# Out-projection operands on another queue, a first block without marks, and a reordered end in a hybrid encoder layer

## The chip, the cores and the metric

The kernel runs on one core of a Trainium2 chip. The metric is the device time of one execution in microseconds (us). Three runs of the kernel before took 2081.64, 2083.21 and 2086.21 us; the median is 2083.21. A profile was taken of a further execution, which took 2080.18 us, with 2078.4 us from its first to its last instruction (the span). All rows of the trace come from that execution.

Engines have short names in the profile: PE is TensorE, PEld its weight loads, DVE VectorE, ACT ScalarE, POOL GpSimd, SP SyncE, which here only issues DMAs. A name with q (SPq, ACTq, POOLq) is the instruction queue of an engine. L207 is line 207 of the kernel.

## What is computed

One layer of an encoder, on two sequences with the same weights: the prompt (512 tokens) and the sample (1024 tokens). The width is 2048, everything is float32.

```
def mixer_layer(x, ...):
    h = rms_norm(x, norm_g)
    c_val, c_glu, c_gate, q, k, v, a_gate = split(h @ w_in)
    q, k = rope(q), rope(k)
    conv_out = conformer_conv(c_val, c_glu, ...) * silu(c_gate)    # 31 taps, layer norm, silu, @ w_pw
    attn_out = banded_sink_attention(q, k, v, sink) * silu(a_gate) # 8 heads, 2 kv heads, window 128
    return x + concat([conv_out, attn_out]) @ w_out

y = rms_norm(mixer_layer(x, ...), final_norm_g)     # for both sequences
```

The final norm divides each row by the root of its mean square and multiplies it by a gain. For the sum `x + ... @ w_out` the kernel must add products to rows that lie in memory; much of the change is about how those rows are fetched.

## The kernel before

**Products.** Each float32 operand is split into a high part and a low part (`parts`, L506: ACT copies the high part, L510, or L514 with a factor; DVE subtracts to get the low part, L511 or L515). A product is then three TensorE passes: high by high, high by low, low by high. For most of the work the blocks are also combined as in Strassen's scheme: seven products P1 to P7 (a `Unit`) in place of eight, on sums of weight blocks and sums of token blocks. One product of a unit is twelve TensorE instructions of 128x512 (L207). The order within a unit is P1, P2, P6, P5, P7, P3, P4 (`ALONE`). P1, P6, P7 and P4 share one bank of the accumulator, so P6 goes on in the bank of P1 after P1's value was taken out (`tap`). The remaining products, those of the prompt's in-projection, are plain (`Job`, L669): 48 instructions each for one block of 128 columns, from two prepared weight blocks.

**Stages.** In order of time: the sample's in-projection as units in four passes (the first by `Plain`, L349); the prompt's in-projection as jobs, with the sample's attention slipped between them (L1167 scores, L1201 transposes, L1196 values); the point-wise product of the convolution for the sample; the sample's out-projection in units of the class `Onto`; then the prompt's point-wise product and its out-projection with the final norm (`LastPost`), written out by hand in `last_run`.

**Onto.** A unit of the out-projection takes a tile from memory for each of its four output quarters (`begin`, L282 to L285, from `x` in the first half of the contraction, from the stored partial sum, `part_out`, in the second), adds the accumulator to it (`tap`, L304) and stores it. A load is asked for `ahead` products before the product that needs it; `ahead` is 2, and 0 for the first two units of the second half, `over[1][:2]`, which run side by side (each product of one, then the same product of the other, on the banks a, b, c and s, s, pt). The unit before asks for the first tile of the next one if `next` is set. The tiles alternate between two rings of four buffers, G and U (`E`, L477). There are 8 pairs of columns, hence 16 units and 64 such loads. They are issued by SP, on whose queue stand nearly all other DMAs as well: weights (L123, L127, L404), token blocks (L878), stores (L504), the attention's queries (L1148).

**Order of the queues.** Each engine works through a list of instructions that is fixed when the kernel is built. The builder goes through the program and takes, for each engine, the ready instruction of highest priority; `urgently` and `high_priority(URGENT)` lift instructions, and `issue_after(i)` keeps an instruction behind `i` on the same engine. `mark` (L523) notes the last DVE and ACT instructions so far, and whatever is built inside `behind()` stays behind these. Lanes (attention, convolution, preparation) are generators that are advanced a little after each group of products (`tick`). An instruction that waits holds up all that stands behind it on its engine.

**Weights.** `w_prep` and `w_prep_now` (L625, L631) prepare the next block: load (`raw`), high and low part (`hl`, three buffers). A `Prep` may be marked `behind`. For the prompt's first job, `pj[0]`, `behind` and `early` are set (L2020), so both its blocks (`k` = 0 and `k` = 8) are made behind the marks. The unit ahead of it, `end = stages[3][-1]` (L2013), looks `NHL - 1` = 2 blocks ahead.

**Landing.** In the last pass of the sample's in-projection a finished quarter is completed by an adding DMA on POOL from the stored part (`add_into`, L501); what follows on it (`done`; for the gates a DVE multiplication, L974, an ACT silu, L982, and a store from ACT's queue, L983) is put in `later` with a count, `landing` = 4. `turn_over` (L542), called once a product, lowers the counts and builds the next step of an entry that has come to zero. Before each job, entries that are left are built at once (L656).

**Start.** `constants` (L561) loads `norm_g` through SP ahead of everything; `first` (L1886) loads the first weights and tokens in small pieces, and 20 spin products (`warm`, L1904, L559) run meanwhile.

**End.** In `last_run`, four row blocks of the prompt (128 rows of 2048) lie in SBUF in two halves (`rows[b][0]`, `rows[b][1]`), each half in interleaved column blocks, even and odd. The last product, P4, adds to the row blocks 2 and 3, one after the other (`finished`, `tap`, `add`, L1726). `complete` (L1728) takes the sum of squares (L1735); on the fourth and last part of a row block it works out the inverse root (L1745 to L1750, a root and one step of correction), scales both halves, each by one ACT and one DVE instruction (L1754, L1756, L1758), and stores each half as it is done (L1759, 512 KB).

Of the kernel before, what the change touches and what calls it, by code (L numbers as in the profile page):

```python
# [7 lines left out]
F32 = mybir.dt.float32  # L8
F32R = mybir.dt.float32r
AF = mybir.ActivationFunctionType  # L10
# [260 lines left out]
class Onto(Unit):  # L271
# [10 lines left out]
    def begin(self, n):  # L282
        if n not in self.d:
            self.d[n] = self.e.E()
            self.e.nc.sync.dma_start(self.d[n], self.source(*n))  # L285

# [99 lines left out]
class Job:  # L386
# [10 lines left out]
    def preps(self, e):  # L397
        def one(k):
# [26 lines left out]

            return Prep(load, make, behind=self.behind)

# [3 lines left out]
class Encoder:  # L431
# [129 lines left out]
    def constants(self):  # L561
# [6 lines left out]

        self.norm_g = load("norm_g", [ND])
        self.ones = self.const.tile([P, P], F32, name="ones")  # L570
# [986 lines left out]
class LastPost(Post):  # L1557
# [136 lines left out]
    def load_rows(self):  # L1694
        e = self.e
        half = D // 2
        self.half = half
        self.rows = [[None, None] for _ in range(NB)]
        self.gain = {}
        self.sq = [e.small(4) for _ in range(NB)]  # L1700
        self.rest = [e.small(1) for _ in range(NB)]
        self.load_columns(0, e.A)

# [24 lines left out]
    def complete(self, b, c, odd):  # L1728
# [5 lines left out]
        junk = e.G().rearrange("p (i x) -> p i x", x=P)  # L1734
        nc.scalar.activation(junk, y, AF.Square, accum_out=self.sq[b][:, n : n + 1])  # L1735
        if n < 3:
            nc.vector.tensor_tensor(y, y, self.gain[c, odd], ALU.mult)
        sq, rest = self.sq[b], self.rest[b]
        if n == 2:
            nc.vector.tensor_tensor(rest, sq[:, 0:1], sq[:, 1:2], ALU.add)  # L1740
            nc.vector.tensor_tensor(rest, rest, sq[:, 2:3], ALU.add)
            nc.vector.tensor_scalar(rest, rest, 1.0 / D, RMS_EPS, ALU.mult, ALU.add)
        if n == 3:
            s, v, t = e.small(1), e.small(1), e.small(1)
            nc.scalar.activation(s, sq[:, n : n + 1], AF.Sqrt, scale=1.0 / D, bias=rest)  # L1745
            nc.vector.tensor_scalar(v, sq[:, n : n + 1], 1.0 / D, rest, ALU.mult, ALU.add)
            nc.vector.reciprocal(s, s)
            nc.vector.scalar_tensor_tensor(t, s, s, v, ALU.mult, ALU.mult)
            nc.vector.tensor_scalar(t, t, -0.5, 1.5, ALU.mult, ALU.add)
            nc.vector.tensor_tensor(s, s, t, ALU.mult)  # L1750
            half = self.half
            for h in range(2):
                other, last = (self.blocks(self.rows[b], h, o) for o in (1 - odd, odd))
                nc.scalar.activation(other, other, AF.Identity, scale=s)  # L1754
                if h == c:
                    nc.vector.scalar_tensor_tensor(last, last, s, self.gain[c, odd], ALU.mult, ALU.mult)  # L1756
                else:
                    nc.vector.tensor_scalar(last, last, s, None, ALU.mult)  # L1758
                nc.sync.dma_start(self.out[b * P : (b + 1) * P, h * half : (h + 1) * half], self.rows[b][h])  # L1759

# [14 lines left out]
    def last_run(self, at):  # L1775
# [5 lines left out]
        for c in range(2):  # L1781
            bank = [None] * 3
            for name in ENDS[c]:
# [25 lines left out]
                if end:  # L1809
# [3 lines left out]
                    parts = {m: e.hl.pop(at + self.place[c, name, m]) for m in self.PAIRS}  # L1813
                    for args in pending:
                        e.urgently(self.complete, *args)
                    pending.clear()
                    for t in range(2):
                        for m in self.PAIRS:
                            for i in range(2):
                                products(t, m, i, parts[m][i])  # L1820
                        finished(t)
                        e.urgently(self.complete, *pending.pop())
                    continue
# [34 lines left out]
def encoder(ctx, tc, a):  # L1858
# [27 lines left out]
    def first():  # L1886
# [16 lines left out]
        e.w_load(3)  # L1903
        e.warm(20, True)  # L1904
        sums = sample.first_sums(x)
# [107 lines left out]
    end = stages[3][-1]  # L2013
    end.look = NHL - 1
    end.before.append(last_before)
# [72 lines left out]
    for u in over[1][:2]:  # L2088
        u.ahead = 0
    over[1][0].next = None  # L2090
# [69 lines left out]
```

## Time and profile before

| what | value |
|---|---|
| timed runs, us | 2081.64, 2083.21, 2086.21 |
| the profiled execution, us | 2080.18 |
| its span, us | 2078.4 |
| mean granted TensorE clock | 0.997 |
| TensorE busy, us | 2060.7 |
| VectorE busy, us | 1754.4 |
| ScalarE busy, us | 1043.6 |
| GpSimd busy, us | 122.6 |
| mean DMA rate, GB/s | 238 |

In the rows of a timeline the first number is the start in us from the beginning of the span, the second the time in us; then engine, line, operation, result <- operands, shape and count of what was merged into the row. In brackets stands the idle time of the engine just ahead of it, and what ended it. A row of waits gives: engine, tile and line that waited, after the arrow what it waited for, then us in total, number of times, and the longest. A row of a stretch gives the busy time of each engine in it, the granted share of TensorE's clock, the share of the DMA engines that was busy, and GB/s. In a list of a line's instructions, three numbers with slashes are minimum, median and maximum, in ns; "DMA to landing" has them in us.

### The profile page before, as it was taken

The page shows a single profiled execution, that of the slowest core. Times are in us where ns is not written, and L with a number is a line of the kernel's source. Part 1 is how long each engine was busy: PE and PEld are TensorE (multiplying, and loading weights), DVE is VectorE, ACT ScalarE, POOL GpSimd, SP SyncE. Part 2 cuts the span into 40 slices and gives each one's busy share as a digit, 9 for nine tenths or more (in the row PEclk, how much of TensorE's full clock was granted, in tenths as well). Part 3 has the DMA queues.
Part 4 walks back from the last instruction along what each step waited for, and adds up shares of the span by engine and source line. Part 5 has one row for each costly group of instructions (what it writes and reads, how often), then busy time and mean ns, then how long its engine had stood idle before and what let it go on. Part 6 is the DMA issues. An engine that isn't in the chain of part 4 may idle for free.

```text
span 2078.4 us, 27092 instructions
## 1 busy us (share of the span) xinstructions
PE 2060.7 (99%) x9259; PEld 1699.2 (82%) x9259; DVE 1754.4 (84%) x2873; ACT 1043.6 (50%) x1711; POOL 122.6 (6%) x176
## 2 busy tenths in 40 slices
PE   9999999999999999999999999999999999999998
PEld 8888888888888888788888888888888887888886
DVE  8767899998899999999666877767799977998887
ACT  7485445333464434554455777336454343454454
POOL 0111111111111111100000000000000000000000
PEclk9999999999999999999999999999999999999999
DMA  8888886864577767954455555996789899678897
GB/s 288 312 298 256 199 223 221 285 220 160 188 242 192 175 169 183 280 166 156 153 172 187 177 182 183 315 330 234 247 289 300 278 299 293 220 247 298 289 333 277
DMA packets 245819, 494.55 MB, mean 238 GB/s; under 512 B 23600, under 2 KB 84400, under 8 KB 245680
## 3 DMA queue, kind: packets, MB, share of 16 engines
q1 hardware_dynamic: 225136, 445.62, 63.9%
q0 software_dynamic: 19392, 45.10, 9.4%
q10 hardware_dynamic: 1152, 2.10, 0.3%
q8 instruction: 72, 1.18, 0.2%
q14 instruction: 67, 0.55, 0.1%
HBM read 331.77 MB, written 160.96 MB: 237 GB/s over the span
## 4 chain that ended last, share of the span: by engine, by line
PE 48%; DVE 7%; issue 6%; DMA 4%; ACT 2%; POOL 1%; SPq 0%; ACTq 0%; POOLq 0%; DVEq 0%
PE a L669 13%; PE a L207 7%; PE c L669 6%; PE b L669 6%; PE c L207 3%; PE pv L1196 2%; PE a L1835 2%; PE s L1167 2%; PE s L1835 2%; PE b L207 1%; PE pt L1201 1%; DVE hl L511 1%; DVE f L1003 1%; DVE t L511 1%; DVE f L1040 1%
## 5 line engine op out<-in xcount | busy, mean ns | idle before, releaser
L207 PE MATMUL a<-t,hl 128*128 128x512 f32 x2640 | 633.6, 391 | 4.7 <-DVE u L304 3.2
L207 PEld LDWEIGHTS a<-t,hl 128*128 128x128 f32 x2640 | 494.7, 188 | 110.6 <-DVE u L304 3.6
L510 ACT ACTIVATE hl<-raw 128x1024 fp32r<-128x1024 f32 (+3 forms) x334 | 296.1, 890 | 384.5 <-PE c L207 81.6
L511 DVE TENSOR_TENSOR hl<-raw,hl 128x1024 fp32r<-128x1024 f32 (+3 forms) x334 | 338.8, 1015 | 145.8 <-ACT hl L510 144.4
L669 PE MATMUL a<-t,hl 128*128 128x512 f32 x1344 | 328.0, 394 | 0.0
L207 PE MATMUL c<-t,hl 128*128 128x512 f32 x1320 | 319.2, 389 | 0.0
L207 PEld LDWEIGHTS c<-t,hl 128*128 128x128 f32 x1320 | 247.3, 188 | 51.6 <-DVE u L304 0.4
L669 PEld LDWEIGHTS a<-t,hl 128*128 128x128 f32 x1344 | 248.6, 188 | 49.8
L1040 DVE SCALAR_TENSOR_TENSOR f<-f,c_w_dw,f 128x512 f32<-128x512 f32 x248 | 173.9, 750 | 0.3
L669 PE MATMUL b<-t,hl 128*128 128x512 f32 x672 | 164.6, 395 | 2.2 <-DVE hl L511 2.2
L1003 DVE SCALAR_TENSOR_TENSOR f<-f,c_w_dw,f 128x512 f32<-128x512 f32 x232 | 163.7, 748 | 1.2 <-ACT f L998 1.2
L669 PE MATMUL c<-t,hl 128*128 128x512 f32 x672 | 164.2, 393 | 0.3 <-DVE hl L511 0.3
L207 PE MATMUL b<-t,hl 128*128 128x512 f32 x660 | 160.0, 389 | 0.0
L669 PEld LDWEIGHTS b<-t,hl 128*128 128x128 f32 x672 | 126.1, 190 | 28.0 <-DVE hl L511 2.6
L669 PEld LDWEIGHTS c<-t,hl 128*128 128x128 f32 x672 | 124.7, 188 | 25.5 <-DVE hl L511 0.7
L207 PEld LDWEIGHTS b<-t,hl 128*128 128x128 f32 x660 | 123.7, 188 | 25.6
L1032 DVE SCALAR_TENSOR_TENSOR f<-f,w_both,f 128x512 f32<-128x512 f32 x120 | 90.0, 750 | 2.1
L236 ACT ACTIVATE u<-a 128x512 f32<-128x512 f32 x82 | 48.7, 594 | 66.8 <-PE a L207 64.2
L236 ACT ACTIVATE g<-a 128x512 f32<-128x512 f32 x78 | 46.3, 594 | 69.1 <-PE a L207 64.6
L1181 ACT ACTIVATE p<-p,tiny 128x384 f32<-128x384 f32 (+1 forms) x96 | 54.5, 570 | 39.8 <-DVE tiny L1178 27.3
L510 ACT ACTIVATE a<-pt 128x512 fp32r<-128x512 f32 x64 | 37.9, 593 | 66.3 <-PE pt L1201 66.2
L511 DVE TENSOR_TENSOR a<-pt,a 128x512 fp32r<-128x512 f32 x64 | 44.1, 689 | 27.3 <-ACT a L510 26.6
(350 smaller groups left out, 2687.9 us busy)
## 6 DMA issues: line engine op xcount, KB each, us to landing
raw<-w_in SPq DMA_DIRECT2D x170, 512.0 KB, 5.3
raw<-w_out SPq DMA_DIRECT2D x31, 512.0 KB, 5.0
raw<-w_pw SPq DMA_DIRECT2D x24, 512.0 KB, 4.2
wsum_P<-raw SPq DMA_DIRECT2D x47, 256.0 KB, 3.3
raw<-wsum_P SPq DMA_DIRECT2D x18, 512.0 KB, 5.0
f<-x_s SPq DMA_DIRECT2D x16, 512.0 KB, 8.2
g<-wsum_P SPq DMA_DIRECT2D x28, 256.0 KB, 4.2
a<-sum_S SPq DMA_DIRECT2D x24, 256.0 KB, 6.2
```

Of the source, the lines that this page charges most:

```text
L207: nc.tensor.matmul(acc, hl[:, l, o, j, :], toks[j][:, r], start=name in FRESH and j == 0 and q == 0, stop=name in LAST and j == HALF - 1 a ...
L236: nc.scalar.activation(t, bank, AF.Copy)
L510: nc.scalar.activation(hi, x, AF.Copy)
L511: nc.vector.tensor_tensor(lo, x, hi.bitcast(F32), ALU.subtract)
L669: nc.tensor.matmul(job.acc[0], hl[:, l, kk // HALF, kk % HALF, :], r, start=i == 0 and p == 0, stop=i == nk - 1 and p == 2,)
L1003: nc.vector.scalar_tensor_tensor(t, h[:, j : j + T], w(j), t, ALU.mult, ALU.add)
L1032: nc.vector.scalar_tensor_tensor(m0, odd[:, j : j + H], both(j), m0, ALU.mult, ALU.add)
L1040: nc.vector.scalar_tensor_tensor(out, d[:, j : j + H], w(2 * j + k), out if j else m0, ALU.mult, ALU.add)
L1167: nc.tensor.matmul(ps[:, 0:n], qs[:, x, h], k[y][:, keys], start=p == 0, stop=p == 2)
L1181: nc.scalar.activation(p[:, 0:n], p[:, 0:n], AF.Exp, bias=nm[:, h : h + 1], accum_out=l[:, h : h + 1])
L1196: nc.tensor.matmul(pv, v[x][:, vs], pt[:, y], start=i == 0 and p == 0, stop=i == last and p == 2)
L1835: nc.tensor.matmul(acc[t], self.toks[name, m][:, x, i, t * P : (t + 1) * P], parts[i][l].rearrange("p a b -> p (a b)"), start=fresh and fi ...
```

## The change

- `Onto.begin`: the tile is loaded by `nc.gpsimd.dma_start` instead of `nc.sync.dma_start`.
- `over[1][:2]`: `ahead` is 1 instead of 0.
- `Job.preps`: only blocks with `k > 0` are `behind`; the first block of `pj[0]` is not.
- `end.landing` is 8 instead of 4.
- `norm_g` is loaded from ACT's queue, and `warm` spins 17 times instead of 20.
- `complete`: the halved sum (`less`) is made beforehand, so that the correction takes one operation fewer after the root; the scaling is a function of its own (`scale`) that is called later. It scales the half that was finished earlier in two contiguous parts, one on DVE and one on ACT, stores these two parts separately (256 KB each), then scales and stores the other half.
- `last_run`: the scaling of row block 0 stays where it was; that of row blocks 1 and 2 is built behind the addition of row block 2's last part on DVE and behind its squares on ACT (`issue_after`), that of row block 3 at the end.

```
 class Onto(Unit):
     def begin(self, n):
         if n not in self.d:
             self.d[n] = self.e.E()
-            self.e.nc.sync.dma_start(self.d[n], self.source(*n))
+            self.e.nc.gpsimd.dma_start(self.d[n], self.source(*n))
...
-            return Prep(load, make, behind=self.behind)
+            return Prep(load, make, behind=self.behind and k > 0)
...
-        self.norm_g = load("norm_g", [ND])
+        self.norm_g = self.const.tile([P, ND], F32, name="c_norm_g")
+        nc.scalar.dma_start(self.norm_g, a["norm_g"])
...
+            nc.vector.tensor_scalar(self.less[b], rest, -0.5, None, ALU.mult)
         if n == 3:
             s, v, t = e.small(1), e.small(1), e.small(1)
             nc.scalar.activation(s, sq[:, n : n + 1], AF.Sqrt, scale=1.0 / D, bias=rest)
-            nc.vector.tensor_scalar(v, sq[:, n : n + 1], 1.0 / D, rest, ALU.mult, ALU.add)
+            nc.vector.tensor_scalar(v, sq[:, n : n + 1], -0.5 / D, self.less[b], ALU.mult, ALU.add)
             nc.vector.reciprocal(s, s)
             nc.vector.scalar_tensor_tensor(t, s, s, v, ALU.mult, ALU.mult)
-            nc.vector.tensor_scalar(t, t, -0.5, 1.5, ALU.mult, ALU.add)
-            nc.vector.tensor_tensor(s, s, t, ALU.mult)
-            half = self.half
-            for h in range(2):
-                other, last = (self.blocks(self.rows[b], h, o) for o in (1 - odd, odd))
-                nc.scalar.activation(other, other, AF.Identity, scale=s)
-                if h == c:
-                    nc.vector.scalar_tensor_tensor(last, last, s, self.gain[c, odd], ALU.mult, ALU.mult)
-                else:
-                    nc.vector.tensor_scalar(last, last, s, None, ALU.mult)
-                nc.sync.dma_start(self.out[b * P : (b + 1) * P, h * half : (h + 1) * half], self.rows[b][h])
+            nc.vector.scalar_tensor_tensor(s, t, 1.5, s, ALU.add, ALU.mult)
+            return lambda: self.scale(b, c, odd, s)
+
+    def scale(self, b, c, odd, s):
+        nc, half = self.e.nc, self.half
+        out = self.out[b * P : (b + 1) * P]
+        x, at = self.rows[b][1 - c], (1 - c) * half
+        nc.vector.tensor_scalar(x[:, : half // 2], x[:, : half // 2], s, None, ALU.mult)
+        nc.scalar.activation(x[:, half // 2 :], x[:, half // 2 :], AF.Identity, scale=s)
+        for h in range(2):
+            cols = slice(h * (half // 2), (h + 1) * (half // 2))
+            nc.sync.dma_start(out[:, at + cols.start : at + cols.stop], x[:, cols])
+        other, last = (self.blocks(self.rows[b], c, o) for o in (1 - odd, odd))
+        nc.vector.scalar_tensor_tensor(last, last, s, self.gain[c, odd], ALU.mult, ALU.mult)
+        nc.scalar.activation(other, other, AF.Identity, scale=s)
+        nc.sync.dma_start(out[:, c * half : (c + 1) * half], self.rows[b][c])
...
-                    for args in pending:
-                        e.urgently(self.complete, *args)
+                    scales = [e.urgently(self.complete, *args) for args in pending]
                     pending.clear()
+                    e.urgently(scales.pop(0))
...
                         finished(t)
-                        e.urgently(self.complete, *pending.pop())
+                        added = nc.cur_bb.bb.instructions[-1]
+                        scales.append(e.urgently(self.complete, *pending.pop()))
+                        squared = self.squared
+                        while scales:
+                            with e.tc.issue_after(added), e.tc.issue_after(squared):
+                                e.urgently(scales.pop(0))
...
-        e.warm(20, True)
+        e.warm(17, True)
...
-    end.look = NHL - 1
+    end.look, end.landing = NHL - 1, 8
...
     for u in over[1][:2]:
-        u.ahead = 0
+        u.ahead = 1
```

More of the change, by code (lines that the diff above doesn't have):

```diff
@@ L1701, in load_rows @@
         self.rest = [e.small(1) for _ in range(NB)]
+        self.less = [e.small(1) for _ in range(NB)]
         self.load_columns(0, e.A)
@@ L1735, in complete @@
         nc.scalar.activation(junk, y, AF.Square, accum_out=self.sq[b][:, n : n + 1])
+        self.squared = nc.cur_bb.bb.instructions[-1]
         if n < 3:
```

## The prediction

> **What bounds the kernel now.** I read the page first, for the busy shares of the engines.
>
> ```profile
> span 2078.4 us, 27092 instructions
> PE 2060.7 (99%) x9259; PEld 1699.2 (82%) x9259; DVE 1754.4 (84%) x2873; ACT 1043.6 (50%) x1711; POOL 122.6 (6%) x176
> ```
>
> TensorE is busy for all but 17.7 us of the span, and the change takes no real product away. So all there is to win is idle TensorE time, plus time at a lowered clock. The second view is the table of stretches. Of 104 stretches of 20 us, two fall far short in the middle of the kernel (columns: PE, weight loads, DVE, ACT, POOL, then granted clock, DMA share, GB/s).
>
> ```profile
> 840.00:860.00 20.00, 16.73 (x73) 13.19 (x72) 19.00 (x29) 17.22 (x29) 3.47 (x4) 1.00 0.97 290
> 860.00:880.00 20.00, 20.00 (x85) 16.41 (x85) 17.90 (x28) 10.12 (x13) 0.88 (x1) 0.91 0.98 303
> 1720.00:1740.00 20.00, 16.77 (x67) 13.39 (x66) 16.05 (x24) 7.07 (x11) 0.00 (x0) 0.91 0.90 295
> ```
>
> The third view, TensorE's own waits, names what ended the idle time there.
>
> ```profile
> PE a L207 <- DVE u L304: 3.2, 1, 3.2
> PE b L669 <- DVE hl L511: 2.2, 1, 2.2
> PE a L207 <- ACT g L236: 1.1, 1, 1.1
> ```
>
> TensorE's timeline places the first two and shows what follows them.
>
> ```profile
> 1708.37 5.60 PE L207 MATMUL a<-t,hl 128*128 128x512 f32 x24
> 1721.97 2.88 PE L207 MATMUL c<-t,hl 128*128 128x512 f32 x12
> 1724.69 1.75 PE L207 MATMUL pt<-t,hl 128*128 128x512 f32 x7
> 1729.67 4.43 PE L207 MATMUL a<-t,hl 128*128 128x512 f32 x12 [3.23 <-DVE u L304]
> ...
> 856.68 0.61 PE L669 MATMUL b<-t,hl 128*128 128x512 f32 x2
> 859.49 12.36 PE L669 MATMUL b<-t,hl 128*128 128x512 f32 x46 [2.19 <-DVE hl L511]
> 877.81 0.89 PE L1167 MATMUL s<-t,a 128*128 128x256 f32 x6
> ```
>
> Twelve products normally take 2.72 us (1721.97 to 1724.69), 0.227 each, and 0.16 for the last to drain. The 46 after the stop at 859 should take 46 x 0.227 + 0.16 = 10.6 and took 12.36: 1.8 us lost to the clock, which the granted clock confirms (0.09 of 20 us). So hole A (859) costs 2.19 + 1.8 = 4.0 us, and hole B (1729) 3.23 + 1.8 = 5.0. [...]
>
> **Hole B: the loads through GpSimd's queue.** The product P6 of a unit accumulates in the bank of P1, so it waits until P1's sum is taken out (L304), and L304 waits for the tile it adds to.
>
> ```profile
> 1721.67 1.75 SPq L878 DMA_DIRECT2D p<-mix_d  x2
> 1723.46 0.43 SPq L285 DMA_DIRECT2D u<-part_out  x1
> ...
> 1728.25 0.63 ACT L510 ACTIVATE t<-p 128x512 fp32r<-128x512 f32 x1 [1.48 <-DMA p<-mix_d]
> 1728.79 0.61 ACT L510 ACTIVATE hl<-g 128x512 fp32r<-128x512 f32 x1
> ...
> 1728.92 0.69 DVE L304 TENSOR_TENSOR u<-a,u 128x512 f32<-128x512 f32 x1 [2.85 <-DMA u<-part_out]
> 1730.13 0.69 DVE L511 TENSOR_TENSOR hl<-g,hl 128x512 fp32r<-128x512 f32 x1
> ```
>
> P1 ended at 1708.37 + 5.60 = 1713.97. Its load was asked for two products before that, but SP issued it at 1723.46, behind token loads that wait for buffers, and it landed 5.5 us later. POOL stands empty in that stretch (0.00 x0 above). After the change all 64 such loads (8 pairs of columns, 2 halves, 4 tiles) go through POOL, where only other loads of this kind stand ahead, each waiting at most for its own G or U buffer. This load's buffer should be free: a unit takes two U tiles in seven products, and there are four. Then L304 runs near 1714.1 and TensorE goes on at 1726.3 instead of 1729.67. What is late next is the first pair's second operand: hl<-g stands on ACT behind a token split that waits for DMA until 1728.25, and its low part ends at 1730.13 + 0.69. P6 of the second unit would want it about 1729.4, and DVE reaches it some 2.9 us sooner because its own wait goes; ACT's wait stays. I take up to 1.2 us given back, 0.6 as the middle: **B = 4.4** (bounds 0 and 5.0).
>
> The cost of a plain load on POOL is not in the trace. POOL has plain stores (L268) and adding loads (L501); the lines under them are the time from issue to landing of L268, of L501, and of these very loads on SP (L285).
>
> ```profile
> L268 POOL DMA_DIRECT2D part_conv<-g x14: 539/539/713, 39.8 to 167.6; - x14
> L501 POOL DMA_DIRECT2D u<-part_conv x16: 856/866/921, 176.1 to 317.1; - x16
> DMA to landing us min/median/max: 2.3/4.3/7.6
> DMA to landing us min/median/max: 3.8/5.5/9.0
> DMA to landing us min/median/max: 2.5/4.2/6.8
> ```
>
> I take 0.54 + 4.3 = 4.8 us, the plain form being nearest, with 0.87 + 9.0 = 9.9 as the far end. A load starts two products ahead of its own (with `ahead` 1 in the paired units, one pair of products, the same 5.4 us, earlier than today's 0), so its sum wants it 3 x 2.72 = 8.2 us later, and TensorE wants the bank some 2 us after that: 10.2. It fits. SP loses 64 issues of 0.43 us and the waits in them; nothing else on SP was binding, so that is costed at nothing.
>
> **Hole A: first block free of the marks, and the landing 8.**
>
> ```profile
> 855.46 1.04 ACT L510 ACTIVATE hl<-raw 128x1024 fp32r<-128x1024 f32 x1
> ...
> 855.74 0.69 DVE L974 TENSOR_TENSOR g<-g,f 128x512 f32<-128x512 f32 x1 [1.00 <-DMA g<-part_gate]
> 858.21 1.22 DVE L511 TENSOR_TENSOR hl<-raw,hl 128x1024 fp32r<-128x1024 f32 x1
> ...
> 865.39 0.63 ACT L510 ACTIVATE a<-u 128x512 fp32r<-128x512 f32 x1 [3.58 <-DMA u<-q_d]
> 866.05 0.69 DVE L511 TENSOR_TENSOR a<-u,a 128x512 fp32r<-128x512 f32 x1 [2.04 <-ACT a L510]
> 876.42 1.22 DVE L511 TENSOR_TENSOR t<-a,t 128x1024 fp32r<-128x1024 f32 x1
> ```
>
> ACT finished its half of the block at 856.5; DVE made the low half only at 858.21, because an L974 ahead of it stood 1.00 us for an adding load. Landing 8 moves that L974 into the next job: 1.7 us off DVE, so L511 can start as ACT ends, 856.55, and be done at 857.8. TensorE wants it at 857.1, so the stop shrinks from 2.19 to about 0.7, without the clock loss (the 1.1 us wait listed above falls into the stretch from 840 to 860, whose clock is 1.00): 1.5 + 1.8 = 3.3 us sooner. Taking the marks off the first block orders it more freely, at no instruction; its bound is the buffer that product P3 frees, so I give it nothing.
>
> But what is late next is close. The attention product at 877.81 needs the low half of the keys, which DVE ended at 876.42 + 1.22 = 877.64: slack 0.2 us. From 866.05 to there DVE works without a gap, and it began at 866.05 because ACT sat on the query load u<-q_d, which takes a U buffer of the unit before. Nothing in the change moves that load. If the order on DVE stays, TensorE arrives 3.3 us early and stands there instead; only the slack, 0.2, is kept. I add a sixth of the other 3.1 for what a newly built order may bring forward: **A = 0.7** (bounds 0.2 - 1.8 = -1.6, if the new stop lowers the clock like the old one, and 4.0).
>
> **Start.**
>
> ```profile
> 0.74 0.39 SPq L566 DMA_DIRECT2D c_norm_g<-norm_g  x1
> 1.19 0.42 SPq L325 DMA_DIRECT2D raw<-w_in  x1
> 1.32 4.53 PE L559 MATMUL pt<-ones_r 128*128 128x128 f32 x20 [1.32 <-DVE ones_r L573]
> 5.65 0.73 PE L349 MATMUL a<-t,hl 128*128 128x512 f32 x1
> ```
>
> Without norm_g every load of SP goes 0.45 us earlier, and so may the first product, at 5.2. Twenty spin products last until 5.85 and would hold it; 17 end 3 x 0.22 = 0.65 sooner, at 5.2. ACT's issue of norm_g costs about what SP's does (0.39), before any weights are there. **0.4** (bounds 0 and 0.45).
>
> **End.**
>
> ```profile
> 2058.74 11.04 PE L1794 MATMUL a<-t,t 128*128 128x512 f32 x48
> 2069.48 0.74 DVE L1756 SCALAR_TENSOR_TENSOR f<-f,tiny,u 128x512 f32<-128x512 f32 x1
> 2070.15 0.68 DVE L1726 TENSOR_TENSOR f<-a,f 128x512 f32<-128x512 f32 x1
> 2072.40 0.15 DVE L1749 TENSOR_SCALAR tiny<-tiny 128x1 f32<-128x1 f32 x1
> ```
>
> TensorE ends at 2069.78, but the last sum starts at 2070.15, when DVE is through with the block before. After the change a block's scaling stands behind the next sum (`issue_after`), so that block is done earlier: 0.3 gained. The root's correction loses one operation on the path (L1749, 0.15 and its start, 0.2 together); the new halved term (`less`) is made off the path. Both halves of a row go to memory in three stores instead of two; the last is still the one of 512 KB, and the added issue on SP runs while ACT still scales. **0.5** (bounds -0.4, if a held-back scaling of 0.75 lands between the root's steps, and 0.9).
>
> **The sum**: 4.4 + 0.7 + 0.4 + 0.5 = 6.0 us. The profiled execution took 2080.18 (1.8 around its span), so 2074.2 for its like; the median of the three timed runs, 2083.21, lies 3.0 above it, and I take the sum from that: **2077.2 us**.
>
> **The rivals.** *A in full*: the rebuilt order puts the keys' split or the query ahead, and 3.3 comes instead of 0.7: 2074.6. For it: DVE idles 2.04 us at 864, enough to work ahead. Against: the slack of 0.2. *B doesn't do what it says*: the load waits on POOL for its buffer and lands as late as now; only 0.7 + 0.4 + 0.5 = 1.6 remains: 2081.6. Against: the buffer count above. *Slower: POOL's loads come late at every unit.* The point is 10.2 us from begin to landing. The slowest rows, 0.87 + 9.0 = 9.9 for an adding load, are just under it; one DVE operation more (0.69) in the way makes 10.6, 0.4 too late, and over 16 units that is 6.4 us, with B (no gain) and the other 1.6: 2083.2 + 6.4 - 1.6 = 2088.0. Against it: from 840 to 860 POOL made four such issues in 3.47 us while DVE was busy for 19.00. [...]
>
> **How the numbers follow.** Forecast 0.45, A in full 0.28, B not 0.16, slower 0.11. Around each I allow 2 us for the spread of timed runs (2081.64 to 2086.21). The range 2072.0 to 2083.5 takes in the first three and leaves out the slower case and the edges. About 0.2% (4.2 us, so 2079.0) is what a measurement of this kernel can tell from no change. Faster: 0.85 x 0.45 + 0.97 x 0.28 + 0.15 x 0.16 = 0.68; slower 0.11; within: 0.21.
>
> **What would show it.** B: in TensorE's waits no L207 behind L304 over 0.5 us, granted clock 1.00 near 1725, and L285 on POOL landing before its P1 ends. A: the stop at the first L669 under 1 us, and then either a stop at the first L1167, L669 or L515 within 20 us (forecast) or none (rival). Start: first L349 product at 5.2. End: last L1726 within 0.1 us of TensorE's end. Wrong would be new stops between 1420 and 1930, where the order of the queues is built anew.

## The result and the profile after

The kernel after takes 2080.12 us (median of 22 runs, 2077.83 to 2084.79), the kernel before on the same chip 2083.18 (22 runs, 2079.72 to 2087.97): a ratio of 0.9986, 95% interval 0.9980 to 0.9992, so 3.1 us faster by the medians (by the ratio 2.9, interval 1.7 to 4.2), half of the 6.0 forecast. On a second chip the ratio was 0.9989 (0.9979 to 1.0000).

The profiled execution of after took 2081.35 us, 1.2 above its median; that of before lay 3.0 below its own. So the two profiles, laid beside each other, show after 1.2 us *slower*. What the change did must be read stretch by stretch. First the head of the page of after:

```profile
span 2079.6 us, 27192 instructions
PE 2061.2 (99%) x9256; PEld 1694.3 (81%) x9256; DVE 1752.1 (84%) x2873; ACT 1043.1 (50%) x1711; POOL 157.8 (8%) x240
```

POOL's 64 new loads account for its 35 us more (64 x 0.55). TensorE's waits in after:

```profile
PE a L207 <- DVE u L304: 1.6, 2, 1.0
PE a L207 <- ACT g L236: 1.2, 2, 1.1
PE s L1168 <- DVE t L511: 1.1, 1, 1.1
PE b L670 <- DVE hl L511: 0.8, 1, 0.8
PE a L670 <- DVE hl L511: 0.5, 1, 0.5
```

The 3.2 us and the 2.2 us are gone; in their place stand several of 0.5 to 1.1. (Lines behind `norm_g` are one higher in after: L669 is L670, L1167 is L1168, L878 is L879; L1726 is L1728, L1759 is L1765 and L1769.) TensorE's timeline of after places them:

```profile
859.43 10.74 PE L670 MATMUL b<-t,hl 128*128 128x512 f32 x46 [0.76 <-DVE hl L511]
871.13 5.99 PE L670 MATMUL a<-t,hl 128*128 128x512 f32 x25 [0.50 <-DVE hl L511]
878.34 0.85 PE L1168 MATMUL s<-t,a 128*128 128x256 f32 x5 [1.11 <-DVE t L511]
...
1547.31 2.30 PE L207 MATMUL a<-t,hl 128*128 128x512 f32 x9 [0.97 <-DVE u L304]
1712.33 5.72 PE L207 MATMUL a<-t,hl 128*128 128x512 f32 x24 [0.63 <-DVE u L304]
1726.54 3.28 PE L207 MATMUL a<-t,hl 128*128 128x512 f32 x12 [0.33 <-ACT hl L510]
1730.87 2.56 PE L207 MATMUL s<-t,hl 128*128 128x512 f32 x10 [0.41 <-DVE hl L511]
```

At 859 the 46 products take 10.74 us, the normal pace; before they took 12.36. Of the 3.23 us that stood at 1729 two stops of 0.33 and 0.41 are left. New are the stops at 871, 878, 1547 and 1712. The loads on POOL, from the list of line 285's instructions in after (four such rows of 16):

```profile
L285 POOL DMA_DIRECT2D u<-part_out x16: 546/546/548, 1690.2 to 1841.9; - x16
...
who waited for it (us, times):
busy tenths in 40 slices 0000000000000000000000000000000111100000
DMA to landing us min/median/max: 2.9/4.8/7.0
```

Nothing waited for any of them: the line under "who waited for it" is already that of the slices. That holds in all eight profiles with these loads on POOL. In the five with them on SP, VectorE waits 3.9 to 6.8 us for them in all. The first one of the second half goes out at 1690.2, where SP issued it at 1723.5.

### A measure for small parts

One execution differs from the next by several us, and the intervals of the timed runs are 2 us and more either way. So each part was also measured inside the profiles: the start of the same TensorE instruction in two profiles, and how much that difference grows over a stretch. The table gives it against the profile of before, in us (negative is faster); the stretches are named by the time of their bounds in before. Kernels are named by their edits; "SP" or "POOL" is the queue of the 64 loads.

| kernel | loads | 0 to 20 | 20 to 850 | 850 to 885 | 1539 to 1715 | 1715 to 1760 | last product to end |
|---|---|---|---|---|---|---|---|
| before | SP | 0 | 0 | 0 | 0 | 0 | 8.63 |
| landing alone | SP | 0.13 | 2.97 | -0.75 | 0.28 | 1.85 | 8.85 |
| end alone | SP | 0.05 | 1.58 | -0.77 | 3.02 | -2.40 | 8.73 |
| start alone | SP | -0.53 | 3.40 | -1.08 | 2.28 | 0.04 | 9.18 |
| after, loads on SP | SP | -1.34 | 2.58 | -1.41 | 1.72 | 0.11 | 8.45 |
| queue alone | POOL | -0.63 | 1.61 | -0.95 | 2.00 | -4.20 | 8.65 |
| queue and end | POOL | 0.14 | 4.00 | -0.61 | 0.71 | -5.07 | 8.58 |
| after | POOL | -0.98 | 1.97 | -0.30 | 3.19 | -3.35 | 8.57 |
| after, second profile | POOL | -1.16 | 1.78 | -0.94 | 2.86 | -3.47 | 8.61 |
| after, old start | POOL | -0.69 | 2.29 | -1.13 | 4.68 | -3.69 | 9.08 |
| after, keys early | POOL | -0.44 | 4.91 | -0.09 | 1.60 | -2.59 | 9.06 |
| after, ahead 0 | POOL | -0.43 | 3.88 | -0.01 | 1.79 | -3.36 | 8.56 |
| after, three edits | POOL | -0.68 | 4.06 | 1.53 | 3.22 | -4.59 | 9.19 |

The column "20 to 850" holds nothing that the change touches, and yet spans 0 to 4.9: that is the noise of one execution, and the profile from which the prediction was worked out is its lowest value. The kernel with the token loads on POOL too (below) is not in the table, since its edit reaches into the out-projection; it has 5.9 in that column, with the clock fallen once at 847 (0.91 granted from 840 to 860).

The rows can be laid beside each other because the edits reach less far than they look. The instruction lists of the engines differ between the kernels only near their edits: the landing moves some operations between 854 and 880; the queue changes the order of the out-projection; the start, but for `norm_g` and three spins, no order at all. Two edits of the change alter no list of any engine: taking the marks off the first block, and `ahead` 1, with the loads on POOL as on SP. So the eight rows with POOL are executions of one order in the out-projection, and the five with SP of another, that of before.

### The profile page after: what moved, and what is told of

It reads as the page before. It is cut to its first block, busy times and chain, and to the rows that moved or that the text cites. A ratio compares the mean times of both kernels' runs of the same rounds, so it can differ in the third digit from the quotient of the medians.

```text
span 2079.6 us, 27192 instructions
## 1 busy us (share of the span) xinstructions
PE 2061.2 (99%) x9256; PEld 1694.3 (81%) x9256; DVE 1752.1 (84%) x2873; ACT 1043.1 (50%) x1711; POOL 157.8 (8%) x240
## 3 DMA queue, kind: packets, MB, share of 16 engines
q8 instruction: 72, 1.18, 0.2%
## 4 chain that ended last, share of the span: by engine, by line
PE 48%; DVE 7%; issue 6%; DMA 5%; ACT 1%; POOL 1%; SPq 0%; ACTq 0%; POOLq 0%; DVEq 0%
PE a L670 12%; PE a L207 6%; PE b L670 6%; PE c L670 6%; PE c L207 3%; PE pv L1197 2%; PE s L1168 2%; PE s L1851 2%; PE a L1851 2%; DVE hl L511 1%; PE b L207 1%; PE pt L1202 1%; DMA a<-ag_d 1%; DVE f L1004 1%; DVE t L511 1%
## 5 line engine op out<-in xcount | busy, mean ns | idle before, releaser
L670 PE MATMUL a<-t,hl 128*128 128x512 f32 x1344 | 328.5, 394 | 0.5 <-DVE hl L511 0.5
L670 PEld LDWEIGHTS a<-t,hl 128*128 128x128 f32 x1344 | 248.5, 188 | 50.8 <-DVE hl L511 0.9
L670 PE MATMUL c<-t,hl 128*128 128x512 f32 x672 | 164.0, 393 | 0.0
L670 PE MATMUL b<-t,hl 128*128 128x512 f32 x672 | 163.1, 392 | 0.9 <-DVE hl L511 0.8
L670 PEld LDWEIGHTS b<-t,hl 128*128 128x128 f32 x672 | 124.9, 188 | 26.5 <-DVE hl L511 1.2
L670 PEld LDWEIGHTS c<-t,hl 128*128 128x128 f32 x672 | 124.7, 188 | 25.0 <-DVE hl L511 0.2
L236 ACT ACTIVATE g<-a 128x512 f32<-128x512 f32 x78 | 46.3, 594 | 70.1 <-PE a L207 65.5
L236 ACT ACTIVATE u<-a 128x512 f32<-128x512 f32 x82 | 48.6, 593 | 65.0 <-PE a L207 63.0
```

The lines of the kernel that those rows point to most:

```text
L236: nc.scalar.activation(t, bank, AF.Copy)
L670: nc.tensor.matmul(job.acc[0], hl[:, l, kk // HALF, kk % HALF, :], r, start=i == 0 and p == 0, stop=i == nk - 1 and p == 2,)
```

## The experiments

**Theory 1**: each part does at its place about what the prediction said, but what TensorE wins is given back within some tens of us, where VectorE or ScalarE works through a list that was built anew; only the loads' queue leaves something over. **Rivals**: a part is worth its forecast and another part eats it up; the gain of hole B comes from asking earlier rather than from the queue; the loads on GpSimd come late.

### The parts alone

*The queue.* The kernel before with

```
-            self.e.nc.sync.dma_start(self.d[n], self.source(*n))
+            self.e.nc.gpsimd.dma_start(self.d[n], self.source(*n))
```

> The kernel before with one edit: the tiles that the out-projection adds to are loaded through GpSimd's queue (ahead stays 0 in the two paired units). Theory 1 (gain at its place, given back by the rebuilt order): TensorE's 3.2 us wait for L304 near 1729 and its clock loss are gone, 4 to 5 us there, but new stops of 1 to 3 us in all appear between 1420 and 1720, because every queue of the out-projection is built anew; the whole is 1.5 to 3.5 us faster. Theory 2 (the part is worth what was forecast, 4.4, and another part of the change takes 3 us): 4 to 5 us faster, no new stops. Theory 3 (the loads on GpSimd come late): VectorE or TensorE waits for the part_out or x loads in the trace, and the time is within 1 us of before or above it.

Measured: ratio 0.9982 (0.9972 to 0.9992), 3.8 us faster. TensorE's timeline of this kernel has

```profile
860.24 10.72 PE L669 MATMUL b<-t,hl 128*128 128x512 f32 x46 [1.45 <-DVE hl L511]
...
1546.09 2.30 PE L207 MATMUL a<-t,hl 128*128 128x512 f32 x9 [0.45 <-DVE u L304]
1728.13 2.56 PE L207 MATMUL s<-t,hl 128*128 128x512 f32 x10 [0.41 <-DVE hl L511]
...
1915.42 11.89 PE L1835 MATMUL a<-hl,t 128*128 128x512 f32 x44 [0.28 <-DVE f L1593]
```

The hole at 1729 is closed (-4.20 from 1715 to 1760) and 2.00 is lost between 1539 and 1715, which the SP rows of the table in part lose too. No load is late, so theory 3 falls. The time itself (1.7 to 5.8 us faster) does not tell theory 1 from theory 2. The row at 860 matters too: this stretch holds the instructions of before unchanged, in the same order, yet the stop is 1.45 us in place of 2.19 and there is no clock loss.

*The landing.* The kernel before with `end.look, end.landing = NHL - 1, 8`.

> The kernel before with one edit: landing 8 for the last unit of the in-projection. Theory 1: the stop at 859 falls from 2.2 us to under 1 us without clock loss, then TensorE waits about 1 us or more at the first scores (L1167) or just ahead of them for VectorE's low parts, and the whole is 0 to 1 us faster. Theory 2 (A is kept): no such stop within 20 us, 2.5 to 3.5 us faster.

Measured: 1.0004 (0.9995 to 1.0012), no gain.

```profile
861.54 10.72 PE L669 MATMUL b<-t,hl 128*128 128x512 f32 x46 [1.15 <-DVE hl L511]
880.01 0.85 PE L1167 MATMUL s<-t,a 128*128 128x256 f32 x5 [1.12 <-DVE t L511]
```

The stop at the first job shrinks and loses no clock, and TensorE then stands 1.12 us at the first scores for the low half of the keys, as theory 1 said. What is left is -0.75 against before's profile. But that profile is the worst of its kind: the four other kernels with the old landing have -0.61 to -1.08 here.

*The end.* The kernel before with the new `complete`, `scale` and their order in `last_run`.

> The kernel before with one edit: the end reordered (halved sum made beforehand, scaling as a function of its own, three stores per row block). Theory 1: from TensorE's last product to the end of the execution 0.3 to 0.9 us less than before, whole 0.5 us faster, within the spread. Theory 2 (the end takes back what the rest wins): 1 us or more later from the last product to the end.

Measured: 0.9996 (0.9985 to 1.0007); from TensorE's last product to the end 8.73 us, before 8.63. Neither the 0.3 to 0.9 of theory 1 nor the loss of theory 2. (How the parts of the end cancel is read below from the profile of after.)

*The start.* The kernel before with `norm_g` on ScalarE's queue and `warm(17)`.

> The kernel before with two edits: norm_g through ScalarE's queue, and 17 spin products in place of 20. Theory 1 (gain of the start is lost before the middle, where VectorE and the DMAs set the pace): the products start 0.6 us sooner and stand 1 us or more ahead at 10 us, and the lead is under 0.3 us by 800; the whole within 0.3 us of before. Theory 2 (kept): 0.4 to 1.5 us faster at the end, the same lead at 800 as at 30.

Measured: 0.9984 (0.9974 to 0.9994), that is 3.3 us faster (1.3 to 5.4), more than either theory said. The profile speaks against it: the products start 0.65 sooner, 0.53 of that is there at 20 us, and at 850 the kernel is 2.87 *behind* the profile of before; its profiled execution took 2089.57, the longest of the eleven. Much of that is one stop far behind the start, in TensorE's timeline and the stretches right behind it:

```profile
1922.48 11.69 PE L1835 MATMUL a<-hl,t 128*128 128x512 f32 x38 [1.08 <-DVE f L1593]
```

```profile
1922.00:1924.00 2.00, 1.52 (x4) 1.24 (x5) 1.97 (x3) 1.53 (x2) 0.00 (x0) 0.50 1.02 341
1924.00:1926.00 2.00, 2.00 (x6) 1.57 (x5) 1.93 (x7) 0.60 (x2) 0.00 (x0) 0.50 1.08 389
1926.00:1928.00 2.00, 2.00 (x6) 1.55 (x5) 1.07 (x3) 1.15 (x2) 0.00 (x0) 0.50 0.57 217
```

The granted clock is 0.50 for 6 us, and with the stop 4.1 us are lost. Theory 2 had to be tried from the other side.

### Parts taken out of the kernel after

*The kernel after, again*, as the measure for the next three.

> The kernel after, unchanged, as the measure for the three kernels beside it on the same chip. Theory 1 (the change is worth 3 us, and one execution differs from the next by 2 us at the same stops): 2 to 4 us faster than before; the stop at 859 again under 1.2 us without clock loss, TensorE again stands about 1 us for VectorE's low parts of the keys at the first scores. Theory 2 (the parts add up to about 7 us as measured one by one, and the first comparison was low): 5 to 7 us faster.

Measured: 0.9989 (0.9979 to 1.0000), 2.3 us faster (0.0 to 4.4). The stops recur at the same places: 0.99 at the first job, 1.11 at the first scores, 0.90 near 1712.

*Without the start's edits.*

> The kernel after with norm_g back on SP's queue and 20 spin products. Theory 1 (the start is worth 0.4 at its place and next to nothing at the end): within 1 us of the kernel after beside it; the products start 0.6 us later, and by 800 us no lead of one over the other that is larger than that of two executions of one kernel. Theory 2 (the start alone brings 3 us): 2.5 to 3.5 us slower than the kernel after beside it.

Measured: 0.9978 (0.9969 to 0.9987), so the kernel without them is, if anything, faster than the one beside it (0.9989). The 3 us of the start alone are not confirmed. In the table, the six profiles with the new start stand at -0.81 on average at 20 us, the six others besides before at -0.28; by 850 they stand at +2.3 and +2.5. The half us is won, and gone.

*The split of the first keys and values ahead on VectorE.*

```
-            e.parts(dst[0], dst[1], held.pop(0))
+            with e.tc.high_priority(SOON if (self.s, g) == (0, 0) else 0):
+                e.parts(dst[0], dst[1], held.pop(0))
```

> The kernel after with the split of the first keys and values at the raised priority of the query's split, so that on VectorE it stands ahead of eight other operations between 868 and 877. Theory 1 (what the landing wins is given back at this chain): no stop at the first scores over 0.3 us, the first scores 1 us sooner relative to the product ahead of them, and 0.5 to 1.5 us faster than the kernel after beside it, unless the postponed operations make a new stop just behind. Theory 2 (TensorE is held there by something else, such as the scores' bank or the query): the stop stays, no gain.

Measured: 0.9985 (0.9977 to 0.9994), no gain over the kernel after. Its timeline on TensorE (lines behind the edit are one higher again):

```profile
880.64 0.89 PE L1169 MATMUL s<-t,a 128*128 128x256 f32 x6
...
885.43 0.62 PE L1169 MATMUL s<-t,a 128*128 128x256 f32 x3 [1.82 <-DVE tiny L1172]
```

The stop for the keys is gone, and nine products later TensorE waits 1.82 us for what VectorE makes of the first scores (L1172), which it now reaches later. VectorE's busy time in that stretch says why (columns as in the table of stretches, here of the kernel after):

```profile
860.00:866.00 6.00, 6.00 (x28) 4.95 (x27) 3.39 (x6) 2.23 (x4) 0.88 (x1) 1.00 1.07 249
866.00:878.00 12.00, 10.73 (x47) 8.30 (x45) 11.83 (x19) 7.64 (x10) 0.00 (x0) 1.00 0.91 326
878.00:884.00 6.00, 5.26 (x27) 4.26 (x28) 6.00 (x14) 0.01 (x1) 0.00 (x0) 1.00 0.74 263
```

From 866 on VectorE works 17.83 of 18 us, and in the six us before it is busy for 3.39: it stands 1.18 us for ScalarE's half of a weight block and 1.54 us for the query that has to be loaded. Moving one of its operations only moves the stop; so the give-back of A looks like a matter of VectorE's total work behind that load. (An earlier query load was not tried.)

*The loads back on SP's queue, `ahead` 1 kept.*

> The kernel after with the out-projection's loads back on SP's queue (ahead stays 1). Theory 1 (the gain of hole B comes from the queue): the stop behind L304 near 1729 comes back with 2 us or more, and the time is 3 to 5 us above the kernel after beside it. Theory 2 (it comes from asking one pair of products earlier): the stop stays away, within 1 us of the kernel after.

Measured: 0.9992 (0.9981 to 1.0003), not to be told from the kernel beside it by time alone. But the timeline decides:

```profile
1731.95 4.45 PE L207 MATMUL a<-t,hl 128*128 128x512 f32 x12 [3.51 <-DVE u L304]
```

The stop is back, with its clock loss (12 products in 4.45 us in place of 2.88), and 1715 to 1760 costs +0.11 where after has -3.35 and -3.47. So the gain comes from the queue and not from the edit `ahead` 1. This run does not test asking earlier, though: with the loads on SP its lists in the out-projection are those of before, and the load goes out at 1725.5, no sooner than there. Whether the same loads, asked for early enough on SP's queue, would do as well was not tried.

### What gives back the gain of hole B

*`ahead` 0 in the kernel after* (`u.ahead = 0` for `over[1][:2]`).

> The kernel after with ahead back at 0 in the two paired units; the loads stay on GpSimd's queue. From the first to the last product of the sample's out-projection it was 332.1 to 333.8 us in three kernels with the old edits there (331.5 in the profile of before), 329.2 with the queue alone, and 330.4 to 332.4 in four profiles with queue and ahead 1. Theory 1 (asking earlier in the pair costs about 2 us, because the new order puts the unit's first token loads later and TensorE stands behind L304 near 1712): 329 to 330 us there, no stop near 1712, and 1 to 2.5 us faster than the kernel after. Theory 2 (the one profile of the queue alone was lucky): 330.5 us or more, the same time as the kernel after.

Measured: 0.9994 (0.9985 to 1.0004), not faster than the kernel after. The stretch took 329.9 us, as theory 1 had it, with a rest of the stop:

```profile
1713.63 5.69 PE L207 MATMUL a<-t,hl 128*128 128x512 f32 x24 [0.20 <-DVE u L304]
```

But theory 1 cannot be right, since the two kernels have the same lists on all engines; this run is one more execution of the kernel after. What it shows is how far one order varies: over the eight profiles with POOL the stop near 1712 is 2.38, 0.90, 0.74, 0.63, 0.24, 0.20 and twice nothing, and the out-projection takes 327.1 to 332.4 us. Theory 1 took four draws on one side for a cause.

*The token loads through POOL as well* (`load_sum` of the out-projection on `nc.gpsimd`, in the kernel after).

> The kernel after with the token sums of the out-projection loaded through GpSimd's queue too, so that they no longer stand behind a weight load and stores on SP's. Theory 1 (the stop near 1712 comes from token loads that are late on SP): the loads for the second half's first product are issued before 1698 and the stop is under 0.3 us; 0.5 to 2 us faster than the kernel after. Theory 2 (the tokens wait for their buffers, or for the memory, not for SP): issued as late as now, the stop stays at 0.6 us or more; or GpSimd's queue, now held by token buffers, delays the tiles, and it is slower.

Measured, in five runs: 1.0043 (1.0029 to 1.0056), 9 us *slower* than before. POOL's timeline:

```profile
1704.71 0.55 POOL L285 DMA_DIRECT2D u<-part_out  x1 [3.31 <-DVE hl L511]
1707.17 0.55 POOL L285 DMA_DIRECT2D g<-xT_s  x1 [1.91 <-DVE hl L511]
1709.29 0.55 POOL L285 DMA_DIRECT2D g<-part_out  x1 [1.57 <-DMA part_out<-g]
1709.88 2.34 POOL L879 DMA_DIRECT2D p<-msum_S  x4
```

Now the token loads stand behind tile loads that wait for a buffer and for a store, and go out at 1709.9 in place of 1698.9. The 1539 to 1715 stretch loses 9.9 us, but these four loads account for at most 1.9 of it, between 1706 and 1715. 7.7 are lost before 1580, where TensorE stops 2.04 us for the attention's scores and 1.55 for its transposes, with the clock at 0.91 from 1540 to 1580; ScalarE waits 4.30 us for a query load there, and what delays that one was not followed. Theory 1 was wrong in this form: SP was not what made the token loads late. The rival mechanism of the prediction (loads late behind others on POOL) does occur, here where loads with different waits stand behind each other on one queue.

What stands ahead of the stop, the profiles of before and after show by themselves. ScalarE in before:

```profile
1702.81 0.63 ACT L510 ACTIVATE t<-p 128x512 fp32r<-128x512 f32 x1 [1.77 <-DMA p<-msum_S]
1703.35 1.05 ACT L510 ACTIVATE hl<-raw 128x1024 fp32r<-128x1024 f32 x1
1705.90 1.99 ACT L510 ACTIVATE t<-p 128x512 fp32r<-128x512 f32 x3 [1.50 <-DMA p<-msum_S]
```

and in after, where TensorE is 3.2 us later at this place:

```profile
1706.15 0.63 ACT L510 ACTIVATE t<-p 128x512 fp32r<-128x512 f32 x1 [1.94 <-DMA p<-msum_S]
1707.31 0.63 ACT L510 ACTIVATE t<-p 128x512 fp32r<-128x512 f32 x1 [0.52 <-DMA p<-msum_S]
1708.14 0.63 ACT L510 ACTIVATE t<-p 128x512 fp32r<-128x512 f32 x1 [0.20 <-DMA p<-msum_S]
1708.67 1.04 ACT L510 ACTIVATE hl<-raw 128x1024 fp32r<-128x1024 f32 x1
```

The weight split hl<-raw stood behind one token split and stands behind three, each with a wait for its own DMA: relative to TensorE it starts 2.2 us later (1708.67 - 3.16 = 1705.5, before 1703.35). VectorE's low half follows it, and L304, which takes out the bank that TensorE wants, stands behind both. At 1547 it is VectorE's own list. Between the low half hl<-g and the row of L304 there, VectorE has in after two rows that in before do not stand there:

```profile
1540.36 2.07 DVE L1004 SCALAR_TENSOR_TENSOR f<-f,c_w_dw,f 128x512 f32<-128x512 f32 x3
1542.34 1.28 DVE L511 TENSOR_TENSOR t<-f,t 128x512 fp32r<-128x512 f32 x2
```

These are 3.3 us of convolution and token splits, and L304 starts at 1546.49 instead of 1543.64. The other profiles bear this out for 1547. With TensorE's own lead or lag taken off, L304 starts at 1543.6 to 1544.4 in the five with SP, none of which stops there; with POOL it starts 0.5 us or more later than that in five of eight, and these are the five that stop (0.27 to 0.99).

For 1712 they bear it out less. No SP profile stops there and six of the eight others do, but L304 is only 0.4 us later with POOL on average (1708.0 against 1707.7, the ranges overlap), and in "end alone", with the old list, the weight split starts 2.1 us later than in before as well. In all thirteen the split starts 0.6 us after the token load that it stands behind has landed (the first with SP, the third with POOL), so the size comes from how late that load lands in the one execution. The SP profiles have stops of their own that the others lack: 0.29 to 1.01 us behind L304 at 1625 in three of five. All this is read from the rows; no kernel was run in which only these orders were restored.

*The queue and the end.* The kernel before with these two parts.

> The kernel before with two edits: the loads through GpSimd's queue and the reordered end; no landing, no ahead, the old start. Theory 1 (the queue is the only part that pays, the end is worth 0 to 0.5): 3 to 5 us faster than before, 329 to 330 us in the sample's out-projection. Theory 2 (the parts need each other): less than 2.5 us.

Measured: 0.9986 (0.9975 to 0.9997), 2.9 us faster, with 327.1 us in the out-projection, the shortest of all. Its time is that of the whole change: start and landing add nothing that can be measured. Its row at 860 shows hole A once more in the unchanged instructions:

```profile
863.57 12.33 PE L669 MATMUL b<-t,hl 128*128 128x512 f32 x46 [2.00 <-DVE hl L511]
```

*A mixture*: the kernel after with the old start, `ahead` 0 and the early keys.

> The kernel after with three edits: the old start, ahead 0 in the two paired units, and the split of the first keys at the raised priority. It keeps what paid in the profiles: the loads through GpSimd's queue, the landing, the end. Measured between the same TensorE instructions as in the other profiles. Theory 1 (the queue is the one part that pays much, 2.6 us net; the rest is worth tenths): from 1715 to 1760 about 3.5 us less than in the profile of before, from 1539 to 1715 1 to 3 us more, from 850 to 885 about 0.5 less; 2 to 4 us faster than before, not to be told from the kernel after. Theory 2 (the parts that were taken out were costing time): 5 us or more faster than before, and no stop over 0.3 us at 1547 and 1712.

Measured: 0.9979 (0.9965 to 0.9992). The hole's stretch gives -4.59, 1539 to 1715 gives back 3.22 with a stop of 0.99 at 1547, and 1.53 is lost from 850 to 885. There the clock fell behind the stop of 1.82 us for L1170; in the kernel with the early keys alone it did not fall behind the same 1.82, and that stretch has -0.09. Its interval holds that of the kernel after, so it is not shown to be better. Theory 2's 5 us lie inside the interval, but its other condition, no stop at 1547, did not hold.

## Why the prediction was half right

The measured 2080.1 lies in the stated range, but that range, up to 2083.5, held the time of before as well. By the number alone it lies nearer to the rival "B doesn't do what it says" (2081.6) than to the forecast (2077.2). It is the stretches, and not the time, that decide against this rival.

**Hole B, 4.4 forecast: right at its place, mis-sized as a whole.** From 1715 to 1760 the five profiles with loads on SP average -0.08 and the eight with POOL -3.79 (-2.59 to -5.07): 3.7 us won, of 5.0 in the hole. The stop for hl<-g that was to give back up to 1.2 came as two of 0.33 and 0.41. But from 1539 to 1715 the SP profiles average +1.46 (0 to 3.02) and the POOL ones +2.51 (0.71 to 4.68): about 1 is given back on average, but the two ranges overlap, so that number is not clear of the noise. Net 2.7, if it is taken. Two steps were off. The term itself was mis-sized, 3.7 for 4.4. And "nothing else on SP was binding, so that is costed at nothing" left out a price: taking 64 instructions off it makes the builder order the lists of TensorE, VectorE and ScalarE in the out-projection anew too, and at 1547 that puts L304 behind operations it had not had ahead. New stops between 1420 and 1930, which the prediction named as the sign of being wrong, did appear, at 1547 and 1712. `ahead` 1, in which the prediction saw 5.4 us of lead, changes no list.

**The rival "POOL's loads come late"**: wrong for the change. An issue takes 0.546 us (0.54 assumed) and lands after 4.8 (4.3 assumed, SP 4.2); 5.4 of the 10.2 us that there are. The far end, 9.9, was not met. All 64 issues take 546 to 580 ns, in a stretch in which VectorE is busy for most of the time (298 of the 330 us from 1540 to 1870).

**Hole A, 0.7 forecast: the mechanism as described, the size 0.1.** With the old landing the stretch 850 to 885 averages -0.68 (five profiles, before's 0 among them), with the new one -0.76 (six, the early keys left out); a difference of 0.1 is nothing beside their spread of 1.1 to 1.4. The stop at the first job shrinks, and TensorE stands at 871 to 878 for VectorE's low halves, in the chain from the query load that the prediction named. Two things in the step were wrong. The hole was read from one execution: 4.0 us there, but 1.45 to 2.00 in four others of the same instructions, and without clock loss in two of them. And the three multiplications that the landing moves (L974, 0.65 each) fall behind the query load, onto the very chain that has no slack. Taking the marks off the first block, given nothing, is nothing.

**Start, 0.4 forecast: 0.5 at its place, 0 at the end.** The first product starts at 5.01 in place of 5.65 (5.2 forecast). By 850 us no difference is left. The step took for granted that TensorE, busy 99% of the time, keeps every lead; over the sample's in-projection the table's 20 to 850 column varies by 4.9 us from one execution to the next, so something other than the start sets the arrival there. A part are single stops behind ScalarE's L236 that come and go: 1.07 us at 85.6 in "start alone" and 1.31 at 630.8 in "after, old start", none of either in before. The rest stays open.

**End, 0.5 forecast: about 0.** Rows of after:

```profile
2071.03 0.69 DVE L1728 TENSOR_TENSOR f<-a,f 128x512 f32<-128x512 f32 x1 [0.55 <-PE a L1805]
...
2074.11 0.71 ACT L1768 ACTIVATE f<-f,tiny 128x512 f32<-128x512 f32 x1
...
2073.99 0.81 SPq L1765 DMA_DIRECT2D y_p<-a  x2
2074.91 0.39 SPq L1769 DMA_DIRECT2D y_p<-f  x1
```

TensorE ends at 2070.99, and the last sum starts 0.04 behind it (0.36 before). The last scaling ends 3.83 behind it (4.33 before), so 0.50 is won, as forecast. But the last store takes 4.65 us from its issue to the end of the span (2074.91 to 2079.56) where it took 4.27 (2074.14 to 2078.41), and is issued 0.09 behind the scaling in place of 0.02: 0.45 goes again. It now follows two stores in place of one; whether that is why it lands later was not tried. "The last is still the one of 512 KB" was true and not enough.

**The sum**: 2.7 + 0.1 + 0 + 0 = 2.8, measured 3.1 (1.7 to 4.2). That they agree so closely is in part luck, since the give-back in the 2.7 is as uncertain as said.

## What to carry to other kernels

- Where a builder orders the queues, moving one class of instructions need not stay local: cost the new lists, by looking at what now stands ahead of each instruction that frees something TensorE wants.
- A stop read from one profile is one draw. Ask how the same instructions fare in other executions before it enters a sum; a profile 3 us below its median has its luck somewhere.
- A lead that TensorE wins may be lost again where the engines that feed it have no idle time behind the place where it was won (at hole A VectorE works 17.83 of the 18 us from 866). Put the DVE and ACT busy shares of the next 20 us beside each gain.

## What was not expected of the hardware

The length of a stop does not decide alone whether the clock falls. At the first job the clock fell behind stops of 1.94, 2.00 and 2.19 us (46 products in 12.33 to 12.36 us) and did not behind 1.48 and less (10.72 to 10.74). At hole B it fell behind 3.23, 3.29, 3.51 and 4.14 us (12 products in 4.43 to 5.49 us), but not behind the 2.38 us of "end alone" (3.06); nor did it behind the 2.38 us at 1713 in "after, old start" (24 products in 5.69 us, in before 5.60 without a stop). Near 1915 it fell behind a stop of 0.28 us (the row with 11.89 us for 44 products, above), behind sixteen 128x1 products that took 1.84 us together; 0.47 and 1.08 us cost 2.3 and 4.1 there. With the token loads on POOL it fell behind 1.55, 1.81 and 2.04 us (granted clock 0.91 over the 20 us from 840, 1540 and 1560). In the mixture it fell behind 1.82 us, and in the kernel with the early keys it did not behind the same 1.82 us at the same place. TensorE's rows, first of the mixture, then of the early keys:

```profile
884.37 0.63 PE L1167 MATMUL s<-t,a 128*128 128x256 f32 x3 [1.82 <-DVE tiny L1170]
...
885.64 4.05 PE L669 MATMUL a<-t,hl 128*128 128x512 f32 x11
```

```profile
885.43 0.62 PE L1169 MATMUL s<-t,a 128*128 128x256 f32 x3 [1.82 <-DVE tiny L1172]
...
886.47 2.70 PE L670 MATMUL a<-t,hl 128*128 128x512 f32 x11
```

The eleven products take 4.05 us in the one and 2.70 in the other. Of these 14 falls ten stand behind stops of 0.28 to 2.19 us. What decides between a fall and none was not shown: no run was made in which only that differed. At hole A, of the five executions with the landing of before, three (1.94, 2.00, 2.19) paid the clock loss, 1.8 us in the profile of before, and two (1.45, 1.48) did not.
